# Fetching the first contraction pair through the software queue with a cast to bf16, in place of fp32 through the hardware queues

## The chip, the cores and the metric

One core of one Trainium2 chip runs the whole kernel. The metric is the device time of one execution in microseconds (us); most executions of a kernel agree within 0.3%. Profiles are of single executions; times in them count from the start of the profiled span, which is about 1.8 us shorter than the measured time. Runs called fast are within 1.5% of the fastest of their kernel.

Names used below: PE is the matrix engine, DVE the vector engine, ACT the scalar engine, POOL the GpSimd engine, SP the sync engine. "Hardware queues" are the DMA queues that SP and ACT issue on, the "software queue" is the one that POOL issues on. Every load with a cast is on the software queue here. A packet is one piece of a load, as the trace lists them.

## The reference

```python
# a: 2048 x 2048, b: 2048 x 2048, gamma: 2048, all fp32; eps = 1e-5
x = np.matmul(a, b)
rms = np.sqrt(np.mean(x ** 2, axis=-1, keepdims=True) + eps)
return (gamma * x / rms).astype(np.float32)
```

## The kernel before

The contraction is cut into 16 tiles of 128, taken in 8 pairs (`kp`). In a head stage the first 4 row blocks of `a` and the left half of `b` are streamed pair by pair: for each pair, 512 rows of 256 columns of `a` (512 KB in memory) and 256 rows of 1024 columns of `b` (1 MB). Pairs 1 to 7 come by the software queue and are cast to bf16 on the way. Pair 0 comes in fp32 by the hardware queues, which need no POOL instruction and start early; its block of `a` is transposed in fp32 and its `b` is cast by DVE and ACT.

```python
a0f = early[:, 0:2048].bitcast(FP32).rearrange("p (r k) -> p r k", r=HB)
b0f = [early[:, 2048 + t * 2048:2048 + (t + 1) * 2048].bitcast(FP32) for t in range(2)]
...
nc.sync.dma_start(out=a0f, in_=a[0:HB * P, 0:W2].rearrange("(r p) k -> p r k", p=P))
for t in range(2):
    nc.scalar.dma_start(out=b0f[t], in_=b[t * P:(t + 1) * P, 0:HALF])
...
def load_b(j, kp):
    nc.gpsimd.dma_start(out=raw[j][kp],
        in_=b[kp * W2:(kp + 1) * W2, j * HALF:(j + 1) * HALF].rearrange("(t p) n -> p t n", p=P))

def load_head(kp):
    nc.gpsimd.dma_start(out=ah(kp),
        in_=a[0:HB * P, kp * W2:(kp + 1) * W2].rearrange("(r p) k -> p r k", p=P))
    load_b(0, kp)
...
load_head(1)
make_identity(nc, identity_f)
for kp in range(2, 4):
    load_head(kp)
...                                     # 11 warm-up matmuls on PE
for kp in range(KP):                    # the head stage; transpose_first() stands before it
    if kp + 4 < KP:
        load_head(kp + 4)
    ...                                 # products of pair kp; transposes of pair kp + 1 in between
```

Of the kernel before, what the change touches and what calls it, by code (L numbers as in the profile page):

```python
# [8 lines left out]
FP32 = mybir.dt.float32  # L9
# [8 lines left out]
def kernel(  # L18
# [13 lines left out]
    nc = tc.nc  # L32
    P = 128
# [4 lines left out]
    W2 = 2 * P  # L38
    MB = M // P
    CH = 512  # L40
    NCH = N // CH
    HALF = N // 2
    HB = 4
# [9 lines left out]
    ps_t = ctx.enter_context(tc.tile_pool(name="ps_t", bufs=1, space=bass.MemoryType.PSUM))  # L53
    ps_a = ctx.enter_context(tc.tile_pool(name="ps_a", bufs=7, space=bass.MemoryType.PSUM))
# [4 lines left out]
    early = consts.tile([P, 6 * 2048], BF16, name="early")  # L59
    head_at = consts.tile([P, KT, HB, P], BF16, name="head_at")  # L60
    raw = [[consts.tile([P, 2, HALF], BF16, name=f"b_{j}_{kp}") for kp in range(KP)]
           for j in range(2)]
# [1 line left out]
    t_right = early.rearrange("p (s k n) -> p s k n", s=3, k=KP)  # L64
    sums = [t_left, t_right]

    a0f = early[:, 0:2048].bitcast(FP32).rearrange("p (r k) -> p r k", r=HB)
    b0f = [early[:, 2048 + t * 2048:2048 + (t + 1) * 2048].bitcast(FP32) for t in range(2)]
    NAH = 6
    ah_slot = [early[:, 6144 + s * 1024:6144 + (s + 1) * 1024].rearrange("p (r k) -> p r k", r=HB)  # L70
               for s in range(NAH)]
# [16 lines left out]
        return (at_even, at_odd)[(mb // 2) % 2][:, mb % 2]  # L88


    nc.sync.dma_start(out=a0f, in_=a[0:HB * P, 0:W2].rearrange("(r p) k -> p r k", p=P))
    for t in range(2):
        nc.scalar.dma_start(out=b0f[t], in_=b[t * P:(t + 1) * P, 0:HALF])

    def ah(kp):
        return ah_slot[(kp - 1) % NAH]

    def load_b(j, kp):
        nc.gpsimd.dma_start(  # L99
            out=raw[j][kp],  # L100
            in_=b[kp * W2:(kp + 1) * W2, j * HALF:(j + 1) * HALF].rearrange(
                "(t p) n -> p t n", p=P))

    def load_head(kp):
        nc.gpsimd.dma_start(  # L105
            out=ah(kp),
            in_=a[0:HB * P, kp * W2:(kp + 1) * W2].rearrange("(r p) k -> p r k", p=P))
        load_b(0, kp)
# [15 lines left out]
    def wait_for(src):  # L124

        nc.gpsimd.tensor_copy(out=pace, in_=src)

    load_head(1)
    identity_f = t_left[:, 2, KP - 1, 0:2 * P].bitcast(FP32)
    make_identity(nc, identity_f)  # L130
# [15 lines left out]

    gamma_sb = consts.tile([P, N], FP32, name="gamma_sb")


    def transpose_first():  # L150
        bank = [ps_t.tile([P, CH], FP32, name="tbank"), ps_a.tile([P, CH], FP32, name="acc")]
        view = [b.rearrange("p (r m) -> p r m", r=HB) for b in bank]
        for t in range(2):
            for r in range(HB):
                nc.tensor.matmul(view[t][:, r, :], a0f[:, r, t * P:(t + 1) * P], identity_f,
                                 is_transpose=True, start=(r == 0), stop=(r == HB - 1))
        for t in range(2):
            cast_first = [lambda: nc.vector.tensor_copy(out=raw[0][0][:, t, :CH],
                                                        in_=b0f[t][:, :CH]),
                          lambda: nc.scalar.copy(out=raw[0][0][:, t, CH:], in_=b0f[t][:, CH:])]  # L160
            move = [lambda h=h: nc.vector.tensor_copy(
                out=head_at[:, t, 2 * h:2 * h + 2, :], in_=view[t][:, 2 * h:2 * h + 2, :])
                for h in range(2)]
            for work in (cast_first + move if t == 0 else move + cast_first):
                work()

    def transpose_head(kp):
        bank = ps_t.tile([P, CH], FP32, name="tbank")
        view = bank.bitcast(BF16).rearrange("p (t r m) -> p t r m", t=2, r=HB)
        for t in range(2):  # L170
            for r in range(HB):
                nc.tensor.matmul(  # L172
                    view[:, t, r, :], ah(kp)[:, r, t * P:(t + 1) * P], identity,
                    is_transpose=True,
                    start=(t == 0 and r == 0), stop=(t == 1 and r == HB - 1),
                )
        nc.vector.tensor_copy(out=head_at[:, 2 * kp:2 * kp + 2, :, :], in_=view)
# [254 lines left out]
    for r in range(HB):  # L432
        x_tile(r, 0)
    early_sums = {4: ((2,), 0, 6), 5: ((5,), 0, 7), 6: ((1,), 0, KP)}
    transpose_first()
    for kp in range(KP):
        if kp + 4 < KP:
            load_head(kp + 4)
# [392 lines left out]
```

## Time and profile before

| | before |
|---|---|
| time, median of 3 runs | 222.53 us (222.32 to 222.62) |
| profiled span | 221.2 us |
| PE busy | 210.0 us, 95% |
| products of pair 0 start | 7.54 us |
| products of pair 1 start | 12.30 us |
| products of pair 4 start | 25.10 us |

Three pieces of the chain of waits of the kernel before (start, length, what held it; both in us). The rows left out are POOL instructions, each under 0.8 us, and matmuls:

```profile
6.70 0.65 POOL early L105
7.35 17.70 DMA b<-in_b_dram
25.05 0.04 issue
25.10 1.67 PE acc L384 x7
...
68.17 139.98 PE acc L289 x648
```

The end of the kernel hangs on a load of `b` that landed at 25.05 us; from there PE works on to 208 us. So anything done in the first 25 us counts only as far as it moves that point. PE's timeline in the kernel before (start, duration, engine, line, instruction, count; in brackets PE's idle time ahead of it and what ended it):

```profile
1.46 4.41 PE L145 MATMUL acc<-sq 128*128 128x512 bf16 x11 [1.46 <-DVE pace L135]
6.40 0.63 PE L155 MATMUL tbank<-t_left,early 128*128 128x128 f32 x4 [0.53 <-DMA early<-in_a_dram]
7.54 2.88 PE L384 MATMUL acc<-b,head_at 128*128 128x512 bf16 x12
...
12.30 1.67 PE L384 MATMUL acc<-b,head_at 128*128 128x512 bf16 x7
...
25.10 1.67 PE L384 MATMUL acc<-b,head_at 128*128 128x512 bf16 x7 [0.85 <-DMA b<-in_b_dram]
```

L145 is the warm-up, L155 the fp32 transposes, L384 the head's products: pair 0 from 7.54, pair 1 from 12.30, pair 4 from 25.10 us. Windows of the kernel before (stretch in us and its length, busy us and instructions by engine, granted PE clock, mean busy share of the DMA engines, GB/s written):

```profile
1.50:3.00 1.50, 1.50 (x4) 0.54 (x5) 0.00 (x0) 1.31 (x2) 1.50 (x3) 1.00 0.71 134
3.00:9.00 6.00, 5.38 (x23) 2.42 (x22) 2.82 (x8) 1.09 (x3) 5.02 (x16) 1.00 0.99 268
9.00:13.00 4.00, 3.60 (x23) 1.66 (x21) 0.82 (x2) 0.91 (x2) 1.23 (x2) 1.00 1.25 207
```

A busy share above 1 means that an engine had more than one packet in flight. The clock column reads 1.00 also where the trace has no clock record: the first one here is at 5.26 us. GB/s here counts bytes written. A load with a cast reads twice what it writes, so 207 GB/s from 9 to 13 us, all casts, is about 414 GB/s of reading, while the 268 before it is mostly fp32, whose reading equals its writing.

Packets by queue in the kernel before (queue, packets, MB, share of the engines' time) at 6 to 7, 7 to 8 and 8 to 9 us, one pair of lines each; q10 is ACT's hardware queue, q0 the software queue. A packet counts with its whole time where it starts, so a share can exceed 100%:

```profile
q10 hardware_dynamic: 46, 0.19, 73.2%
q0 software_dynamic: 14, 0.01, 5.2%
...
q10 hardware_dynamic: 54, 0.19, 53.5%
q0 software_dynamic: 78, 0.04, 28.9%
...
q0 software_dynamic: 363, 0.19, 136.7%
q10 hardware_dynamic: 12, 0.01, 4.2%
```

POOL issued the first software load at 1.25 us, but the queue's first packet starts at 6.27 us, and it moves next to nothing until the hardware queue has run out at about 8 us.

### The profile page before, as it was taken

The page shows a single profiled execution, that of the slowest core. Times are in us where ns is not written, and L with a number is a line of the kernel's source. Part 1 is how long each engine was busy: PE and PEld are TensorE (multiplying, and loading weights), DVE is VectorE, ACT ScalarE, POOL GpSimd, SP SyncE. Part 2 cuts the span into 40 slices and gives each one's busy share as a digit, 9 for nine tenths or more (in the row PEclk, how much of TensorE's full clock was granted, in tenths as well). Part 3 has the DMA queues.
Part 4 walks back from the last instruction along what each step waited for, and adds up shares of the span by engine and source line. Part 5 has one row for each costly group of instructions (what it writes and reads, how often), then busy time and mean ns, then how long its engine had stood idle before and what let it go on. Part 6 is the DMA issues. An engine that isn't in the chain of part 4 may idle for free.

```text
span 221.2 us, 3022 instructions
## 1 busy us (share of the span) xinstructions
PE 210.0 (95%) x1035; PEld 97.7 (44%) x1035; DVE 167.4 (76%) x330; ACT 128.1 (58%) x263; POOL 29.4 (13%) x59
## 2 busy tenths in 40 slices
PE   7899899999999999999999999999999999999950
PEld 2445454444455444444444444444444444444430
DVE  2428789999988898969696639855794759797691
ACT  3110001830698898678945997389738995334570
POOL 7634323220000001200110002000200000000040
PEclk9999999999999999999999999999999999999996
DMA  6999999999938596956799249955798349044045
GB/s 184 223 202 209 203 208 210 211 211 238 426 114 357 187 291 120 316 230 150 219 308 397 79 88 266 367 221 95 187 302 367 69 90 381 32 190 193 1 190 191
DMA packets 36321, 47.13 MB, mean 213 GB/s; under 512 B 21969, under 2 KB 26065, under 8 KB 34897
## 3 DMA queue, kind: packets, MB, share of 16 engines
q0 software_dynamic: 9936, 23.33, 41.7%
q1 hardware_dynamic: 25936, 22.29, 33.6%
q10 hardware_dynamic: 432, 1.31, 2.0%
q8 instruction: 8, 0.13, 0.2%
q14 instruction: 9, 0.07, 0.1%
HBM read 34.60 MB, written 16.78 MB: 232 GB/s over the span
## 4 chain that ended last, share of the span: by engine, by line
PE 83%; DMA 8%; POOL 3%; DVE 2%; issue 1%; ACT 1%; DVEq 0%; ACTq 0%; POOLq 0%
PE acc L289 69%; PE acc L384 12%; DMA b<-in_b_dram 8%; POOL early L105 1%; POOL b L99 1%; DVE x L709 1%; PE tbank L415 1%; PE tbank L172 1%; DVE x L712 1%; ACT sq L307 0%; PE tbank L189 0%; PE acc L189 0%; DVE a L709 0%; ACT sq L778 0%; DVE x L786 0%
## 5 line engine op out<-in xcount | busy, mean ns | idle before, releaser
L289 PE MATMUL acc<-b,s 128*128 128x512 bf16 x408 | 92.1, 379 | 0.0
L289 PEld LDWEIGHTS <-s 128*128 128x128 f16 (+1 forms) x512 | 49.9, 98 | 59.9 <-DVE s L264 0.4
L384 PE MATMUL acc<-b,head_at 128*128 128x512 bf16 x176 | 41.9, 379 | 1.0 <-DMA b<-in_b_dram 0.9
L307 ACT ACTIVATE sq<-x 128x512 bf16<-128x512 f32 x54 | 34.0, 630 | 6.9 <-DVE x L709 3.0
L366 DVE SCALAR_TENSOR_TENSOR x<-x,r,gamma_sb 128x1024 f32<-128x1024 f32 x28 | 34.8, 1281 | 0.7
L223 ACT ACTIVATE sq<-a 128x1024 bf16<-128x1024 f32 x24 | 25.3, 1054 | 2.4 <-DMA a<-in_a_dram 1.9
L384 PEld LDWEIGHTS <-head_at 128*128 128x128 bf16 x176 | 16.8, 98 | 20.6 <-issue 1.9
L246 ACT ACTIVATE head_at<-a,s 128x2048 f16<-128x2048 f32 x10 | 20.0, 1998 | 3.7 <-DVE s L233 3.7
L426 ACT COPY x<-acc 128x512 f32<-128x512 f32 x6 | 3.4, 586 | 25.7 <-PE acc L384 25.7
L289 PEld LDWEIGHTS <-head_at 128*128 128x128 f16 (+1 forms) x112 | 10.9, 98 | 13.2
L289 PE MATMUL acc<-early,head_at 128*128 128x512 bf16 x64 | 14.5, 379 | 0.0
L289 PEld LDWEIGHTS <-at_even 128*128 128x128 f16 x96 | 9.4, 98 | 11.3
L289 PE MATMUL acc<-early,s 128*128 128x512 bf16 x56 | 14.4, 379 | 0.0
L264 DVE TENSOR_TENSOR s<-head_at 128x1024 f16<-128x1024 f16 (+5 forms) x22 | 13.4, 635 | 0.1
L596 DVE TENSOR_TENSOR x<-x,x 128x512 f32<-128x512 f32 x9 | 6.2, 692 | 8.8 <-ACT x L594 8.3
L99 POOL DMA_DIRECT2D b<-in_b_dram x15 | 10.6, 706 | 16.0 <-DMA b<-in_b_dram 13.4
L578 ACT COPY x<-acc 128x512 f32<-128x512 f32 x9 | 5.2, 574 | 11.6 <-PE acc L289 11.5
L289 PE MATMUL acc<-t_left,s 128*128 128x512 bf16 x48 | 11.3, 379 | 0.0
L280 DVE TENSOR_TENSOR b<-b 128x1024 bf16<-128x1024 bf16 x16 | 10.8, 684 | 0.2
L289 PE MATMUL acc<-t_left,head_at 128*128 128x512 bf16 x48 | 10.9, 379 | 0.0
L289 PE MATMUL acc<-t_left,at_even 128*128 128x512 bf16 x48 | 10.8, 379 | 0.0
L289 PE MATMUL acc<-early,at_even 128*128 128x512 bf16 x48 | 10.8, 379 | 0.0
(111 smaller groups left out, 216.7 us busy)
## 6 DMA issues: line engine op xcount, KB each, us to landing
out_dram<-x SPq DMA_DIRECT2D x30, 512.0 KB, 3.8
a<-in_a_dram POOLq DMA_DIRECT2D x10, 1024.0 KB, 8.7
b<-in_b_dram POOLq DMA_DIRECT2D x15, 512.0 KB, 17.5
a<-in_a_dram POOLq DMA_DIRECT2D x4, 512.0 KB, 16.6
early<-in_a_dram POOLq DMA_DIRECT2D x7, 256.0 KB, 14.8
early<-in_b_dram ACTq DMA_DIRECT2D x2, 512.0 KB, 5.9
gamma_sb<-in_gamma_dram POOLq DMA_DIRECT2D x1, 1024.0 KB, 14.8
early<-in_a_dram SPq DMA_DIRECT2D x1, 512.0 KB, 5.5
```

The costliest lines, as they stand in the source:

```text
L99: nc.gpsimd.dma_start(out=raw[j][kp], in_=b[kp * W2:(kp + 1) * W2, j * HALF:(j + 1) * HALF].rearrange("(t p) n -> p t n", p=P))
L223: nc.scalar.activation(out=junk, in_=a32[mb][:, h * HALF:(h + 1) * HALF], func=ACTF.Square, scale=2.0 ** -8, accum_out=n2[:, h:h + 1])
L246: nc.scalar.activation(out=a16[mb], in_=a32.pop(mb), func=ACTF.Copy, scale=factor.pop(mb))
L264: nc.vector.tensor_tensor(out=sum_of(g, s)[:, lo:hi, :], in0=x[:, lo:hi, :], in1=y[:, lo:hi, :], op=op)
L280: nc.vector.tensor_tensor(out=flat[:, 1:3, :], in0=flat[:, 1:3, :], in1=flat[:, 0::3, :], op=ALU.add)
L289: nc.tensor.matmul(bank, lhsT[:, kp, :], rhs, start=(start and kp == 0), stop=(kp == KP - 1), skip_group_check=not start)
L307: nc.scalar.activation(out=sq[:, 0:CH], in_=src, func=ACTF.Square, scale=inv_sqrt_n, accum_out=msq[mb][:, c:c + 1])
L366: nc.vector.scalar_tensor_tensor(out=x, in0=x, scalar=inverse_of[mb], in1=gamma_sb[:, h * HALF:(h + 1) * HALF], op0=ALU.mult, op1=ALU.mult)
L384: nc.tensor.matmul(bank, head_at[:, kt, r, :], head_rhs(c, kt), start=(kt == 0), stop=(kt == KT - 1))
L426: copy(out=x_chunk(*g), in_=banks[g])
L578: nc.scalar.copy(out=c, in_=one[1])
L596: nc.vector.tensor_tensor(out=t, in0=t, in1=x12, op=ALU.add)
```

## The change

The intent: pair 0 takes the road of the other pairs. That removes four casts from DVE and ACT, the fp32 transposes from PE, and half of the bytes written.

```diff
-    nc.sync.dma_start(out=a0f, in_=a[0:HB * P, 0:W2].rearrange("(r p) k -> p r k", p=P))
-    for t in range(2):
-        nc.scalar.dma_start(out=b0f[t], in_=b[t * P:(t + 1) * P, 0:HALF])
+    a0 = early[:, 0:1024].rearrange("p (r k) -> p r k", r=HB)

     def ah(kp):
-        return ah_slot[(kp - 1) % NAH]
+        return ah_slot[(kp - 1) % NAH] if kp else a0
...
+    nc.gpsimd.dma_start(out=ah(0), in_=a[0:HB * P, 0:W2].rearrange("(r p) k -> p r k", p=P))
+    for t in range(2):
+        nc.gpsimd.dma_start(out=raw[0][0][:, t, :], in_=b[t * P:(t + 1) * P, 0:HALF])
     load_head(1)
...
-    def transpose_first():              # fp32 transposes, moves, casts on DVE and ACT
-        ...
-    transpose_first()
+    transpose_head(0)
```

More of the change, by code (lines that the diff above doesn't have):

```diff
@@ L65 @@
     sums = [t_left, t_right]
-    a0f = early[:, 0:2048].bitcast(FP32).rearrange("p (r k) -> p r k", r=HB)
-    b0f = [early[:, 2048 + t * 2048:2048 + (t + 1) * 2048].bitcast(FP32) for t in range(2)]
     NAH = 6
@@ L147 @@
     gamma_sb = consts.tile([P, N], FP32, name="gamma_sb")
-    def transpose_first():
-        bank = [ps_t.tile([P, CH], FP32, name="tbank"), ps_a.tile([P, CH], FP32, name="acc")]
-        view = [b.rearrange("p (r m) -> p r m", r=HB) for b in bank]
-        for t in range(2):
-            for r in range(HB):
-                nc.tensor.matmul(view[t][:, r, :], a0f[:, r, t * P:(t + 1) * P], identity_f,
-                                 is_transpose=True, start=(r == 0), stop=(r == HB - 1))
-        for t in range(2):
-            cast_first = [lambda: nc.vector.tensor_copy(out=raw[0][0][:, t, :CH],
-                                                        in_=b0f[t][:, :CH]),
-                          lambda: nc.scalar.copy(out=raw[0][0][:, t, CH:], in_=b0f[t][:, CH:])]
-            move = [lambda h=h: nc.vector.tensor_copy(
-                out=head_at[:, t, 2 * h:2 * h + 2, :], in_=view[t][:, 2 * h:2 * h + 2, :])
-                for h in range(2)]
-            for work in (cast_first + move if t == 0 else move + cast_first):
-                work()
     def transpose_head(kp):
```

## The prediction

> **What bounds the kernel now.** PE is busy 210.0 of 221.2 us (engine table). The chain of waits has three parts: 7.35 us of POOL issues, 17.7 us of DMA (pair 4's b tile, landing at 25.05 us), then PE without a gap until 208.2 us, and a tail. So the change can only shift the 25.05. Before it (timeline): warm-up matmuls to 5.87 us, fp32 transposes at 6.40, products from 7.54, a wait for pair 1's b tile (products at 12.30), steps of 3.9 us, then 0.85 us of wait for pair 4's b tile. A step's 16 products (0.216 us apart) and 8 transposes (0.45 us) take 3.9 us; the DMA delivers a pair in about 3.9 us too (205 to 210 GB/s written, in the windows). So what pair 1 gains or loses reaches the end.
>
> **What changes.** Removed: eight fp32 transposes (1.15 us of PE), four moves (0.38 us each) and four casts (0.43 to 0.74 us) on DVE and ACT; added: eight bf16 transposes (0.45 us), one copy (0.69 us). This is off the limit, as PE waits for pair 1 anyway. Three issues (0.9, 0.7, 0.7 us) now stand ahead on POOL; the identity comes at 5.9 us instead of 3.7, just as the warm-up ends.
>
> What counts is the DMA start. HBM reads are the same; a cast halves what is written. Before, the hardware queues move 1.57 MB of fp32 from 1.75 to 8.2 us. The software queue, issued at 1.25 us, shows no packet before 6.2 us and comes up at 7.5 to 8.2 us, as the hardware queue ends (packets by queue in 1 us windows). The Trainium skill, "DMA: Bandwidth & Descriptors", section "Queues, rings and completion order", says that each engine goes round its queues by whole packets; I read the late start as that, not as a slow software queue. Later loads, with idle engines, show a first packet 1.2 us after issue.
>
> From its real start (about 7.9 us, mean over engines) the queue landed a1 1.5 us later and b1 4.0 us later; PE used b1 0.45 us after that. With pair 0 ahead (1.3+2.6 us), PE starts pair 1 at F+8.25, F being the mean start. Break-even with 12.30 is F = 4.05 us. My F: 1.25 + 0.94 (first issue) + 0.67 (rest of the 1.2) + 0.75 for slow first packets (about 1 us each on idle engines) = 3.6 us. Gain about 0.45 us at pair 1, and the same at pair 4, whose extra 1 us (a 16 KB instruction fetch falls there) stays.
>
> **Prediction.** 222.1 us, range 220.9 to 224.2. Faster by over 2% 0.01, within 2% 0.96, slower 0.03. PE could save at most the 2.3 us by which it lags its own pace at 25.1 us.
>
> **Signs.** First software packets at about 3 us; bf16 transposes at 6; first products at 7; pair 1's at 11.9 (12.30 before); pair 4's at 24.7 (25.1); the last matmul earlier by the same; no new PE wait after 26 us; DMA near 205 GB/s from 4 us on.
>
> **What would make it wrong.** The software queue's first start may itself be slow (its late start fits that too): first packets at 5 to 6 us make everything 1 to 2 us later, 223.5 to 224.7, and let PE idle after the warm-up. If the hardware queues' slow first packets came from HBM or b's layout, the new start is slow as well. If the 16 KB fetch falls where there is slack, 0.8 us more is won.

## The result, and the profile after

| | before | after |
|---|---|---|
| time, median of 4 runs | 222.57 us (222.32 to 222.65) | 224.0 us (223.53 to 224.21) |
| profiled span | 221.2 us | 222.2 us |
| products of pair 0 start | 7.54 us | 7.24 us |
| products of pair 1 start | 12.30 us | 13.70 us |
| products of pair 4 start | 25.10 us | 25.68 us |
| last products (half banks) start | 211.43 us | 212.19 us |

The ratio is 1.0063, 95% interval 1.0048 to 1.0078. (Ratios here are the mean time of one kernel's fast runs over that of the other's of the same rounds, so not quite the ratio of the quoted medians.) The change makes the kernel 0.6% slower, which is within 2% but clear of noise.

PE's timeline of the changed kernel, to be read against the one of before; L155 is now the bf16 transpose and L367 the head's product:

```profile
5.84 0.61 PE L155 MATMUL tbank<-identity,early 128*128 128x128 bf16 x8
7.24 1.69 PE L367 MATMUL acc<-b,head_at 128*128 128x512 bf16 x7 [0.79 <-DVE head_at L160]
9.58 1.24 PE L367 MATMUL acc<-b,head_at 128*128 128x512 bf16 x5 [0.66 <-DMA b<-in_b_dram]
11.05 0.62 PE L155 MATMUL tbank<-identity,early 128*128 128x128 bf16 x8 [0.23 <-DMA early<-in_a_dram]
...
13.70 1.46 PE L367 MATMUL acc<-b,head_at 128*128 128x512 bf16 x6 [0.65 <-DMA b<-in_b_dram]
...
25.68 1.67 PE L367 MATMUL acc<-b,head_at 128*128 128x512 bf16 x7
```

The transposes and the first half of pair 0 are in good time, even earlier than before. Then PE waits for pair 0's second half of `b` (9.58 us) and for pair 1. (Where seven products read x6, the trace has lost a record; the x5 at 9.58 us is whole, since pair 1's transposes stand after twelve products.) The chain of waits of the changed kernel:

```profile
1.24 0.94 POOL early L125
2.18 0.52 POOL b L127
2.70 6.84 DMA b<-in_b_dram
9.54 0.29 issue
9.83 15.80 DMA b<-in_b_dram
25.63 0.04 issue
25.68 1.67 PE acc L367 x7
```

A load of pair 0's `b`, its second half, 0.5 MB in memory, was issued from 2.70 us on and takes until 9.54 us. It now stands in the chain. The same windows of the changed kernel:

```profile
1.50:3.00 1.50, 1.50 (x4) 0.53 (x5) 0.00 (x0) 0.72 (x2) 1.50 (x3) 1.00 0.01 2
3.00:9.00 6.00, 5.13 (x23) 2.14 (x22) 1.05 (x3) 0.00 (x0) 5.92 (x18) 1.00 1.13 142
9.00:13.00 4.00, 2.84 (x17) 1.23 (x17) 0.69 (x1) 0.00 (x0) 1.68 (x3) 1.00 1.23 203
```

From 3 to 9 us it is all casts: 142 GB/s written, 284 GB/s read, against 406 after 9 us. With 6 us at 142 and 1.5 us at 2, about 855 KB are written by 9 us, so about 1710 KB read. Before, 1.5 us at 134 and 6 us at 268 give about 1809 KB written, 1573 KB of it fp32 and so 236 KB of casts, which is 1573 + 2 x 236 = 2045 KB read. The changed kernel is 335 KB of reading behind at 9 us. At 410 GB/s that is 0.8 us.

The packets of pair 0 in the two traces give the sum:

| | before | after |
|---|---|---|
| first packet of pair 0 | 1.80 us | 2.91 us |
| end of pair 0's last packet | 8.30 us | 9.25 us |
| time for pair 0 | 6.5 us | 6.3 us |
| pair 1's `b` complete on the first engine, on the last | 11.42, 11.90 us | 11.91, 13.18 us |

Pair 0 takes nearly the same time by either road, though the cast halves what is written; the changed kernel only starts 1.1 us later. Another 0.33 us comes from pair 1, whose `b` completes over 1.3 us of engine spread instead of 0.5. This sum describes the two traces. It does not show that an earlier start would win the 1.1 us back; experiment 6 tried that, and it did not.

Of the 1.40 us at pair 1, 0.58 us are left at pair 4: there the kernel before waited 0.85 us for its load. The last products are 0.76 us late and the span 1.0 us. The last 0.24 us lie in the tail: SP issued the last store 0.50 us after its data in the changed kernel and 0.08 us after it before. The 0.50 us is there again in experiment 1; nothing was run on it, so its cause is open. The profiled execution of before was itself 0.4 us above its kernel's median, which is why the spans differ by 1.0 and the medians by 1.4 us.

### The profile page after: what moved, and what is told of

The parts are those of the page before. It is cut to its first block, busy times and chain, and to the rows that moved or that the text cites. A ratio compares the mean times of both kernels' runs of the same rounds, so it can differ in the third digit from the quotient of the medians.

```text
span 222.2 us, 2992 instructions
## 1 busy us (share of the span) xinstructions
PE 208.8 (94%) x1015; PEld 97.3 (44%) x1035; DVE 165.4 (74%) x325; ACT 126.8 (57%) x261; POOL 31.2 (14%) x62
## 4 chain that ended last, share of the span: by engine, by line
PE 82%; DMA 10%; DVE 2%; issue 1%; ACT 1%; POOL 1%; DVEq 0%; ACTq 0%; POOLq 0%
PE acc L272 68%; PE acc L367 12%; DMA b<-in_b_dram 10%; DVE x L692 1%; PE tbank L398 1%; PE tbank L155 1%; ACT sq L290 1%; DVE x L695 1%; POOL early L125 0%; PE tbank L172 0%; PE acc L172 0%; DVE a L692 0%; POOL b L127 0%; ACT sq L761 0%; DVE x L769 0%
## 5 line engine op out<-in xcount | busy, mean ns | idle before, releaser
L367 PE MATMUL acc<-b,head_at 128*128 128x512 bf16 x171 | 41.3, 379 | 2.4 <-DMA b<-in_b_dram 1.3
L367 PEld LDWEIGHTS <-head_at 128*128 128x128 bf16 x176 | 16.8, 98 | 21.9 <-issue 2.5
L160 DVE COPY head_at<-tbank 128x1024 bf16<-128x1024 bf16 x8 | 5.5, 686 | 8.8 <-PE tbank L155 8.8
L263 DVE TENSOR_TENSOR b<-b 128x1024 bf16<-128x1024 bf16 x16 | 10.8, 684 | 0.2
L123 POOL COPY pace<-x 128x1 f32<-128x1 f32 x4 | 1.6, 412 | 65.9 <-DVE x L588 64.7
L272 PE MATMUL acc<-early,at_even 128*128 128x512 bf16 x48 | 10.8, 379 | 0.1
```

The costliest lines, as they stand in the source:

```text
L160: nc.vector.tensor_copy(out=head_at[:, 2 * kp:2 * kp + 2, :, :], in_=view)
L263: nc.vector.tensor_tensor(out=flat[:, 1:3, :], in0=flat[:, 1:3, :], in1=flat[:, 0::3, :], op=ALU.add)
L272: nc.tensor.matmul(bank, lhsT[:, kp, :], rhs, start=(start and kp == 0), stop=(kp == KP - 1), skip_group_check=not start)
L367: nc.tensor.matmul(bank, head_at[:, kt, r, :], head_rhs(c, kt), start=(kt == 0), stop=(kt == KT - 1))
```

## The experiments

The main question was why pair 0's packets are slow. In the changed kernel a packet of `b` (4 KB read, 2 KB written) took 172 to 173 ns in pair 1, without exception, and 173 to 174 ns on average in the pairs after it, but 258 ns on average in pair 0, up to 1236 ns. Times of experiments are medians; "look" is a single execution. The kernel before, run beside them, was at 222.53 to 222.78 us. Several kernels also had PE at half clock for a while; that is taken up in experiment 2.

**1. The changed kernel again (a look).**

The edit: none.

> The changed kernel once more, as the control of the slow stretch. In the first look the packets of pair 0's two b loads took 173 ns at first, then 200 to 700 ns (some over 1000) from 5.3 to 8.9 us, against a steady 173 ns for those of pair 1. If the slow stretch belongs to the kernel, it is there again: pair 0's second b load lands at about 9.2 us, PE starts pair 1 near 13.7 us. If it was a chance of one execution, pair 0 lands near 7.6 us and pair 1 starts near 11.6 to 11.9 us.

Measured: 223.65 us; pair 0's second half landed at 9.41 us and PE waited for `b` four times, 2.3 us in sum. Pair 0's `b` packets took 260 ns on average. The slow stretch belongs to the kernel.

**2. Pair 0's `b` in one load (3 rounds).**

```diff
-    for t in range(2):
-        nc.gpsimd.dma_start(out=raw[0][0][:, t, :], in_=b[t * P:(t + 1) * P, 0:HALF])
+    load_b(0, 0)
```

> Pair 0's b tile comes in one load of two rows per partition, as every other pair's, in place of two loads of one row each. Shape theory (the loads of one row per partition are what reads slowly): packets at 173 ns throughout, pair 0's b tile lands at about 7.7 us, PE starts pair 1 at about 11.9 us, time about 1.5 us below the changed kernel, 222.3 to 222.7. Rows theory (these 256 rows of b read slowly) and time theory (something in the first 9 us slows 4 KB reads): still slow, pair 1 near 13.7 us, about 224.0 us.

Measured: 226.95 us, ratio 1.0227 (1.0186 to 1.0269). Its packets of pair 0 were as slow (261 ns), so the shape is not it. But the time was 3 us worse than the changed kernel, which no theory had. Here the two halves of the load show their worth. PE's timeline and windows of this kernel:

```profile
11.00 4.11 PE L366 MATMUL acc<-b,head_at 128*128 128x512 bf16 x12 [3.86 <-DMA b<-in_b_dram]
...
10.00:11.00 1.00, 0.00 (x1) 0.00 (x1) 0.00 (x0) 0.00 (x0) 0.00 (x0) 0.69 1.27 209
11.00:12.00 1.00, 1.00 (x3) 0.40 (x3) 0.00 (x0) 0.00 (x0) 0.70 (x1) 0.50 1.18 217
```

With nothing to do for 3.86 us, PE lost its clock (third number from the right: 0.69, then 0.50), and the twelve products took 4.11 us; the kernel before did them in 2.88. The Trainium skill, "TensorE: Matmul & The Clock Gate", section "Part 1: The HAM clock gate", says that PE falls to half clock after an idle window of about 3.4 us and that the window runs freely. The trace agrees in the length: the granted clock changed at 6.96, 10.38 and 13.79 us, 3.41 us apart, and PE worked for only 0.2 us in the first of these stretches. How idle PE must be is another matter: the last section has runs that differ. With the load in halves, no wait of PE in the changed kernel is longer than 0.8 us and the clock stays at 1.00.

**3. Pairs 0 and 1 exchanged in memory (a look; the result is wrong, as later blocks were not exchanged).** All loads of the head and of `b` take rows 256 to 511 where they took 0 to 255, and the reverse.

```diff
     def load_b(j, kp):
-        ... in_=b[kp * W2:(kp + 1) * W2, ...]
+        ... in_=b[swap(kp) * W2:(swap(kp) + 1) * W2, ...]   # swap: 0 -> 1, 1 -> 0, else kp
     # the same for the head's a, and in the three loads of pair 0
```

> Pairs 0 and 1 exchanged in memory for the head and for b (rows 256 to 511 of b first, then rows 0 to 255); the result is wrong on purpose. Rows theory: the first pair's loads run at 173 ns and the second's are slow. Shape theory and time theory: the first pair's are slow again from 5.3 to 9 us, pair 1's are at 173 ns.

Measured: 223.75 us, relative error 0.61. The first pair was slow again (255 ns on average) and the second ran at 173 ns. It is not the rows.

**4. `b` ahead of `a` on the queue (a look).**

```diff
-    nc.gpsimd.dma_start(out=ah(0), in_=a[0:HB * P, 0:W2].rearrange("(r p) k -> p r k", p=P))
     for t in range(2):
         nc.gpsimd.dma_start(out=raw[0][0][:, t, :], in_=b[t * P:(t + 1) * P, 0:HALF])
+    nc.gpsimd.dma_start(out=ah(0), in_=a[0:HB * P, 0:W2].rearrange("(r p) k -> p r k", p=P))
```

> On the software queue pair 0's two b loads go ahead of its a load. Time theory: the b packets run at 173 ns from 3 to 5.3 us, and what follows from 5.3 to 9 us (a0, a1 and b1) is slow. Shape theory and rows theory: the b packets are slow right away or after the first few, also at 3 to 7 us, and all that follows is at its usual 60 and 173 ns. Pair 1 starts near 13.5 us in both, as the same bytes stand ahead of it.

Measured: 228.03 us, with PE 3.6 us idle and half clock until 15.96 us. The windows:

```profile
2.50:5.00 2.50, 2.50 (x7) 0.88 (x6) 0.00 (x0) 0.00 (x0) 2.42 (x5) 1.00 0.84 125
5.00:9.00 4.00, 1.09 (x4) 0.15 (x1) 0.36 (x2) 0.00 (x0) 4.00 (x14) 1.00 1.10 122
9.00:13.00 4.00, 2.50 (x12) 1.35 (x13) 0.69 (x1) 0.00 (x0) 1.66 (x3) 0.52 1.24 204
```

`b` was slow from its first packet at 2.69 us (214 ns on average in its first half), which no pure "5 to 9 us" theory allows, and the loads of `a` behind it were somewhat slow as well until 9 us (80 ns a packet for the first, against 60 later), which neither the shape nor the rows allow.

**5. The first issue delayed by 4 us (a look).** Five 128x1024 memsets on POOL ahead of the first load.

```diff
+    for n in range(5):
+        nc.gpsimd.memset(x_slot[n], 0.0)
     nc.gpsimd.dma_start(out=ah(0), in_=a[0:HB * P, 0:W2].rearrange("(r p) k -> p r k", p=P))
```

> The changed kernel with five 128x1024 memsets on POOL ahead of its first issue, so that the first load starts some 6 to 9 us later; nothing else changes. The slow stretch of pair 0's b loads is not a matter of shape (one load: slow too) nor of rows (pairs exchanged: slow too), and with b first it was slow from its first packets at 2.3 us and a0 and a1 after it were slow to 8.7 us. Clock-on-the-wall theory (something in the first 9 us of the execution takes memory or fabric from the loads): the b packets now run at 173 ns, from the first to the last, and pair 0 lands 4.5 us after the first packet. First-megabytes theory (the first loads of b are slow whenever they come): the same 200 to 700 ns packets, pair 0 landing 6.5 us after the first packet. The time itself is longer by the delay and by a slow PE clock, and means nothing.

Measured: 227.98 us; the first packet came at 6.83 us. The windows:

```profile
7.00:9.00 2.00, 0.00 (x0) 0.00 (x0) 0.00 (x0) 0.00 (x0) 1.93 (x5) 0.89 1.24 177
9.00:13.00 4.00, 2.68 (x12) 1.43 (x13) 1.05 (x3) 0.00 (x0) 4.00 (x14) 0.50 0.96 116
13.00:17.00 4.00, 3.95 (x19) 1.75 (x18) 0.44 (x1) 0.00 (x0) 1.61 (x3) 0.70 1.24 204
```

The slow stretch (116 GB/s) moved with the loads: 9 to 13 us, where the changed kernel reads at full rate. It is not a matter of time since the kernel started.

**6. Only the `b` half of the change (3 rounds).** `a0` in fp32 by the hardware queue with its fp32 transposes; pair 0's `b` by the software queue.

```diff
+    nc.sync.dma_start(out=a0f, in_=a[0:HB * P, 0:W2].rearrange("(r p) k -> p r k", p=P))
...
-    nc.gpsimd.dma_start(out=ah(0), in_=a[0:HB * P, 0:W2].rearrange("(r p) k -> p r k", p=P))
...
-    transpose_head(0)
+    transpose_first()                   # as in the kernel before, without the casts of b
```

> Only the b half of the change: a0 stays on the hardware queue in fp32 with fp32 transposes, pair 0's b halves come by the software queue with a cast. Bytes on all queues are as before, but the hardware queue uses the engines from 1.75 us on, 1.1 us before the software queue can. If the loss of the change is the engines' idle start plus a slow stretch that ends at about 9 us whatever is loaded: pair 0's second half lands at about 8.2 us, pair 1 starts at about 12.5 us, 222.5 to 223.2 us. If the loss came from a0's bf16 route or the later identity: as the kernel before or better, under 222.3. If the loss is the b loads' being on the software queue: as the changed kernel, 223.7 to 224.2.

Measured: 224.2 us, ratio 1.0060 (1.0043 to 1.0078), the same loss as the whole change. The engines worked from 1.85 us on, but the first packet of `b` came at 3.32 us and pair 0's `b` still landed only at 9.30 us; PE waited 2.30 us and ran at half clock from 9.3 to 12.7 us. The expectation had pair 1 at 12.5 us; it started at 15.40. The profiled execution was the slowest of four (225.1 us, mean clock 0.979; the others 223.56 to 224.29 us, 0.989 to 0.993), so how much of the median is the clock's is not known. Of the three outcomes named beforehand, the time is that of the third: the loss comes with `b` on the software queue. That the loss is the engines' later start is not borne out: with the early start the landing is 9.30 us, against 9.54 in the changed kernel and 8.2 expected.

**7. Only the `a` half of the change (3 rounds).** `a0` by the software queue with bf16 transposes; pair 0's `b` in fp32 by the hardware queue.

```diff
+    for t in range(2):
+        nc.scalar.dma_start(out=b0f[t], in_=b[t * P:(t + 1) * P, 0:HALF])
...
-    for t in range(2):
-        nc.gpsimd.dma_start(out=raw[0][0][:, t, :], in_=b[t * P:(t + 1) * P, 0:HALF])
...
-    transpose_head(0)
+    for t in range(2):
+        nc.vector.tensor_copy(out=raw[0][0][:, t, :CH], in_=b0f[t][:, :CH])
+        nc.scalar.copy(out=raw[0][0][:, t, CH:], in_=b0f[t][:, CH:])
+        if t == 0:
+            transpose_head(0)
```

> Only the a half of the change: a0 by the software queue with bf16 transposes, pair 0's b stays on the hardware queue in fp32 with casts on DVE and ACT. If engines take whole loads in turn, a0 goes between the two b loads (from 4 to 5.5 us), a0 lands at about 6 us and pair 1 starts near 12.3 us, so that the time is that of the kernel before, 222.3 to 222.8. If the transposes' route costs something itself: 223.5 or more.

Measured: 227.06 us, ratio 1.0194 (1.0179 to 1.0209), a clear miss. `a0` did not go between the two hardware loads. Packets by queue at 4 to 5 us (first line) and 5 to 6 us (last two):

```profile
q10 hardware_dynamic: 75, 0.27, 88.6%
...
q10 hardware_dynamic: 50, 0.17, 61.4%
q0 software_dynamic: 76, 0.04, 36.4%
```

The software queue, issued at 1.25 us, got its first packet at 5.31 us, just as the first engine had finished both hardware loads. PE then waited 2.93 us for `a0`, and its twelve first products took 4.21 us at the cold clock (in the profiled execution the full clock came only at 14.05 us, so the warm-up had not brought it). Since the changed kernel's software queue starts at 2.91 us when the hardware queues are empty, its late start before is shown to be a matter of the hardware loads, as the prediction said. By what rule the engines choose is not shown: here the software queue got no turn between two hardware loads, while in the kernel before its packets ran from 6.27 us on, beside a hardware load that no engine had finished before 7.67 us. Both hardware loads of `b`, alone on the engines at first, took 4.7 us for 1.05 MB, with packets of 224 ns on average and never under 156. So a slow beginning is not the software queue's alone, nor the cast's.

**8. `a0` on the hardware queue and `b` in one load (a look).**

```diff
# against experiment 6
-    for t in range(2):
-        nc.gpsimd.dma_start(out=raw[0][0][:, t, :], in_=b[t * P:(t + 1) * P, 0:HALF])
+    load_b(0, 0)
```

> As the b half alone, with pair 0's b in one load. PE then has fp32 transposes at about 6 us and waits for the whole b tile. If the large loss of the one-load version of the changed kernel (227 us) was PE's clock, which fell to one half after PE had waited 3.9 us, then here it depends on that wait alone: b lands near 8.5 to 9 us, a wait under 3 us, clock full, 222.5 to 223.5 us. If one load of b is itself slow, about 226 us again with the clock full.

Measured: 226.66 us. PE waited 4.50 us for `b` and lost its clock; pair 0's packets took 280 ns. The expected landing of 8.5 to 9 us came near 10.8 us, so neither outcome of the expectation fits as written.

**9. and 10. POOL waits for pair 0 before it issues pair 2 (3 rounds each),** in the changed kernel and in the version of experiment 6. In most runs so far the slow stretch had ended with POOL's burst of back-to-back issues, and this ends the burst after pair 1.

```diff
+    gate = consts.tile([P, 1], FP32, name="gate")
+    nc.gpsimd.tensor_copy(out=gate, in_=raw[0][0][:, 1, HALF - 1:HALF])
     for kp in range(2, 4):
         load_head(kp)
```

> The changed kernel with one POOL copy that waits for pair 0's second b half to land before the loads of pairs 2 and later are issued; pair 1's loads stay queued, so the engines do not run dry. With the start delayed by 4 us the slow stretch came 4 us later with it, so it belongs to the start of the loads, not to the clock on the wall. In most of these kernels it ends where POOL's burst of eight back-to-back issues ends. Burst theory (POOL's writing of descriptors, issue after issue, slows the reads): b packets at 173 ns from 5 us on, pair 0 lands at about 7.7 us, pair 1 starts at about 11.9, time 221.9 to 222.6 us. Warm-up theory (the first 2 MB or first 6 us of loads are slow whoever issues what): slow packets to about 8.9 us as before, pair 0 lands at about 9.3, 223.7 to 224.5 us.

> The same wait in the version with a0 in fp32 on the hardware queue and pair 0's b on the software queue. Burst theory: a0 lands at 4 us, pair 0's b at about 6.8 us, pair 1's at about 10.5 us, PE's clock stays full, 220.8 to 221.6 us, faster than both kernels. Warm-up theory: pair 0's b lands at about 9 us again, 223.5 to 224.5 us.

Measured: 226.65 us, ratio 1.0181 (1.0159 to 1.0202), and 225.81 us, ratio 1.0150 (1.0120 to 1.0181). The windows of the first:

```profile
5.00:9.00 4.00, 3.21 (x19) 1.51 (x17) 1.05 (x3) 0.00 (x0) 0.29 (x1) 1.00 1.08 133
9.00:13.00 4.00, 3.17 (x19) 1.28 (x18) 0.69 (x1) 0.18 (x1) 3.70 (x14) 1.00 1.21 200
13.00:19.00 6.00, 4.23 (x24) 1.93 (x24) 0.73 (x2) 0.41 (x1) 3.36 (x5) 1.00 1.11 158
```

POOL was idle from 5.3 to 9.3 us (0.29 us busy, the end of the identity), and the reads were as slow as ever (133 GB/s against 129 in the changed kernel): the burst theory falls. The surprise is the third line. From 13 us on the reads are slow a second time, where the changed kernel shows 207 GB/s (the line below), and the slow load is that of pair 2, which the gate had made late. Neither "the first 2 MB" nor "the first 6 us" explains that.

```profile
13.00:19.00 6.00, 5.30 (x31) 2.69 (x31) 1.82 (x4) 0.59 (x1) 2.16 (x3) 1.00 1.25 207
```

**11. and 12. Pair 0's `b` in four column chunks, 1 KB a packet (3 rounds each),** in the changed kernel and in the version of experiment 6; the identity is made before pair 1's loads.

```diff
-    for t in range(2):
-        nc.gpsimd.dma_start(out=raw[0][0][:, t, :], in_=b[t * P:(t + 1) * P, 0:HALF])
+    for c in range(4):
+        cols = slice(c * 256, (c + 1) * 256)
+        nc.gpsimd.dma_start(out=raw[0][0][:, :, cols],
+                            in_=b[0:W2, cols].rearrange("(t p) n -> p t n", p=P))
```

> The changed kernel with pair 0's b loaded in four column chunks of 256, so that each packet reads 1 KB, as those of a do, in place of 4 KB; POOL makes the identity before pair 1's loads. Waiting to issue did not help (slow to 9 us again, and the loads after the wait slow as well), so neither POOL's burst nor the start of the execution is the cause by itself. In all runs so far the early packets of 1 KB reads run near their usual 60 ns (65 on average) while those of 4 KB take 258 ns on average in place of 173. Packet theory (only the long reads suffer early): the chunks run at 60 to 70 ns, pair 0 lands at about 7.3 us, pair 1 starts at 11.9 to 12.2 us, time 222.1 to 222.7 us. Amount theory (the first 2 MB after a start are slow however they are read): the chunks take 90 to 100 ns, pair 0 lands after 8.7 us, 223.5 us or more.

> The same chunks with a0 in fp32 on the hardware queue, which starts 1.1 us earlier. Packet theory: pair 0's b lands at about 6.6 us, pair 1's products start at 11.3 to 11.6 us, PE's clock stays full, time 221.2 to 222.0 us, faster than both kernels. Amount theory: pair 0's b lands at 8.5 us or later, 223 us or more.

Measured: 225.81 us, ratio 1.0137 (1.0120 to 1.0155), and 225.17 us, ratio 1.0099 (1.0066 to 1.0132). The windows of the first:

```profile
5.00:9.00 4.00, 2.56 (x13) 1.19 (x10) 1.05 (x3) 0.00 (x0) 3.92 (x8) 1.00 1.09 124
9.00:11.00 2.00, 0.81 (x4) 0.31 (x5) 0.00 (x0) 0.00 (x0) 2.00 (x12) 0.92 1.34 202
11.00:13.00 2.00, 2.00 (x6) 0.75 (x5) 0.00 (x0) 0.00 (x0) 1.47 (x2) 0.50 1.12 165
```

124 GB/s from 5 to 9 us: short packets do not help. The packet theory had their duration right: the chunks' packets took 70 and 64 ns on average in the two kernels, against the usual 60, so short reads lose far less than long ones. But it overlooked that four packets of 60 ns are 240 ns for the 4 KB that one packet of `b` reads in 173 ns, and pair 0 landed at 10.14 us. The amount theory had the landing and the time right and the packets (90 to 100 ns) wrong, and it falls on the last line: with 2 MB read by 10 us, pair 1's `b` was still slow, at 200 ns a packet against 173 in the changed kernel. The chunks had delayed its issue.

**What the fourteen profiles have in common.** For every load of `b` on the software queue, up to pair 4, I set the mean duration of its packets against its lead: the median start of its packets minus the end of its issue on POOL. There are 74 such loads.

| lead | loads | mean packet of a load |
|---|---|---|
| 1.8 to 5.4 us | 22 | 200 to 317 ns |
| 6.3 to 13.8 us | 52 | 173 to 174 ns |

None breaks the split. Three lines of the list, lead and mean packet in the order of issue (the first two entries of the first two are pair 0's halves, then pairs 1 and 2; in the third, pair 0 came in chunks and the list begins with pair 1):

```
after    2.6us:225ns  4.1us:292ns  6.5us:173ns  8.4us:173ns
gated    2.5us:218ns  3.9us:282ns  6.3us:173ns  4.2us:209ns
b0_1k    4.4us:200ns  7.3us:173ns  9.7us:173ns
```

The gate moved pair 2 from 8.4 us of lead to 4.2 and from 173 to 209 ns; the chunks moved pair 1 from 6.5 to 4.4 us and from 173 to 200 ns. So a load of `b` runs at full rate here if it was issued some 6 us before it runs, and slower if not. The first megabytes of a kernel can't have that lead. This was found by looking back over the runs, and the late-issued loads (pair 2 in the two gated kernels, pair 1 in the two chunked ones) are its only test.

Later loads of the same traces show that it is a regularity of these `b` loads and not a rule for all. At 64.33 us the kernel before issues a 1 MB load of `a` (8 KB a packet, no cast) while the DMA engines are idle. Its first packet comes 1.25 us later, its first 16 packets take 813 ns on average, its last 32 take 309. So a slow beginning is not peculiar to the start of a kernel. (Whether it is the same one is not shown: in the changed kernel `b`'s first packets ran at 172 to 175 ns, and the slow ones came after 5 us.) The next load, issued at 66.69 us while the first is running, has a lead of only 2.8 us and yet takes 314 ns a packet. In all fourteen traces the first of these two loads takes 343 to 402 ns a packet, the second 314 to 323. There a load onto idle engines is slow, and the one behind it is not. But in the gated kernel pair 2 was slow although pair 1's loads were still running when it was issued. What the queue does in these microseconds the traces don't show. Time since issue, the number of loads ahead at the issue, and the time since POOL's issues resumed go together in the `b` loads; what tells them apart stays open.

No version tried was faster than the kernel before.

## Why the prediction was right or wrong

The measured 224.0 us lies in the range of 220.9 to 224.2 us, near its upper end, and "within 2%" was right. The direction was wrong: a gain of 0.4 us was forecast, and 1.4 us were lost. That the range holds the result is due to its width, and not to the mechanism.

- **"This is off the limit" (the removed casts and fp32 transposes).** Right. Pair 0's products began at 7.24 instead of 7.54 us, and PE waited for loads afterwards all the same.
- **The start of the software queue.** Better than said: the first packet at 2.91 us, against "about 3 us", with a mean start near 3.2 us by my estimate from the first completions against a forecast F of 3.6. That the old start at 6.2 us was due to the hardware loads is shown by this. The mechanism, engines going round their queues, is not: in experiment 7 the software load did not get its turn between two hardware loads, though in the kernel before software and hardware packets did run side by side from 6.27 us.
- **"With pair 0 ahead (1.3+2.6 us)": the failed step.** The 3.9 us were the steady rate of later pairs. Pair 0 took 6.3 us, hardly less than the 6.5 us of the fp32 loads, and the sign "DMA near 205 GB/s from 4 us on" failed with it (142 GB/s from 3 to 9 us). I had read the hardware loads' slow 6.4 us as their own fault and expected the software queue to be free of it. The 0.75 us that I allowed for slow first packets was for the queue's first ones; the slow packets of `b` came after 5 us, up to 9 us. The warning sign stood in the profile before (low DMA shares at 6 to 8 us), and was named among what could go wrong ("HBM or b's layout"), though not with these causes: rows and shape are excluded by experiments 2 and 3. Against the 6.5 us of before, halving the writes bought 0.2 us, and the later start stands beside it with 1.1 us. But experiment 6, with the early start kept for `a0`, lost as much (ratio 1.0060 against 1.0063). So moving pair 0's `b` is enough for the loss; why its first packets are slow stays open.
- **"What pair 1 gains or loses reaches the end."** Half right: of 1.40 us at pair 1, 0.58 us were left at pair 4, because the kernel before had 0.85 us of waiting there, which the prediction had itself noted.
- **"No new PE wait after 26 us."** Right as far as the trace shows: PE's list of waits has none. The later start of the last store in the tail (0.24 us) was not foreseen.
- **"Let PE idle after the warm-up".** In the changed kernel the clock stayed full. But experiments 2, 4 to 6, 8, 11 and 12 show how near that edge the head is; in 7 the profiled execution had no full clock before 14 us.

## What to carry to other kernels

Do not price the first loads of a kernel at the rate of its steady state: read the rate of the first megabytes from the profile before, and ask what makes it low before expecting another queue to be free of it. Loads put on idle engines later in the kernel began slowly here as well. A queue that looks late may only be waiting behind another. Do not count on halving the bytes written: here it bought 0.2 of 6.5 us. Look at PE's clock wherever PE waits for data: after waits of 1.6 to 4.5 us these kernels ran at half clock for 3.4 to 6.8 us. Feeding PE in halves kept the clock in the changed kernel, feeding it in quarters (experiments 11 and 12) did not.

## What the Trainium skill lacked or had wrong

- "DMA: Bandwidth & Descriptors": it gives a fixed cost and a rate per transfer, but nothing on a slow beginning. Here packets of `b` took 200 to 317 ns on average with a lead of at most 5.4 us between issue and running, and 173 to 174 ns from 6.3 us on. Hardware loads of the same data took 224 and 228 ns on average, with a least packet of 156. A 1 MB load onto idle engines at 64 us took 813 ns a packet at first and 309 at its end.
- "DMA: Bandwidth & Descriptors", section "Queues, rings and completion order": engines are said to go round their queues by packets of descriptors. In experiment 7 a software load issued by 2.19 us got its first packet at 5.31 us, behind two hardware loads. These had 256 pieces, 16 for each of the 16 engines if shared evenly, so the trace can't tell whether the page is wrong or one turn was that long.
- "DMA: Bandwidth & Descriptors", section "Latency and other measured facts": about 1 us to the first byte on the software path. Here it was 1.7 us from the start of the first issue (1.24 to 2.91 us), 0.73 us from its end, and 1.25 us from the start of the issue at 64.33 us, 0.73 us from its end.
- "TensorE: Matmul & The Clock Gate", section "Part 1: The HAM clock gate": one idle window of about 3.4 us is said to halve the clock. In experiment 6 a wait of 2.30 us for data, behind fp32 transposes, was followed by 3.41 us at half clock. In experiment 11 the clock halved at 10.68 us, though PE had worked on products for 0.9 us of the 3.41 us before and no wait in them was longer than 1.6 us.
